# Rotary queries kept in memory as eight blocks of 128 rows, written in four parts, in place of two blocks of four times 128 rows

## The chip, the cores and the metric

The kernel runs on one core of a Trainium2 chip. The metric is the device time of one launch in microseconds. Three runs of the kernel before gave 2459.61, 2461.49 and 2461.84 us; the median is 2461.49 us. The profiled execution took 2459.21 us.

## The reference, cut to what matters

One step of a two-layer decoder on 1024 prompt tokens and 64 sample tokens (8 sequences of 8). Layer A mixes by pooling; layer B attends to one shared latent of 256 numbers and one rotary key of 64 numbers per token. Each of the 8 heads has a query of two parts: 128 numbers without position (the latent is multiplied to match) and 64 rotary ones.

```python
cq = _rmsnorm(u @ w_dq, q_norm)
q = jnp.einsum('btr,rhe->bthe', cq, w_uq)
q_lat = jnp.einsum('bthn,rhn->bthr', q[..., :QK_NOPE], w_uk)
return q_lat, _rope(q[..., QK_NOPE:], pos)
...
s = (jnp.einsum('bqhr,bkr->bhqk', q_lat, c)
     + jnp.einsum('bqhe,bke->bhqk', q_rope, kr)).astype(jnp.float32) * SM_SCALE
```

The prompt's queries attend causally to the prompt; the sample's queries attend to 8 pages of 128 cached tokens each, and to their own tokens. Everything is in float32.

## The kernel before, in words

All activations lie with features on the 128 partitions and tokens on the free axis; the 1088 tokens are cut into chunks of 384, 384 and 320 (`CH`). Matrix products run as three passes of split float32 numbers, a rounded high part and the rest as a low part (`mm3`, lines 188 to 190). A `Plan` holds the list of steps, and loads weight pieces into a ring ahead of their use (`load_piece`, lines 157 and 168). The tile framework places every semaphore. Nearly all DMAs are issued by SyncE (SP), in the order of the program, and SP waits at an issue until what it needs is there; ScalarE issues a few of its own (line 930).

`qkv_phase` computes the shared latent and key, the query's low rank part, and then the queries. `qnope(hh, c, w)` makes one head's no-position query for one chunk: VectorE multiplies the product by the reciprocal norm into an `hl` tile (line 753; four buffers), and SP writes it to memory, to `qn_d[hh]` (line 755). `qrope(g, c, w)` makes the rotary queries of four heads (group `g`) for one chunk. Its two products hold, on 128 partitions, 32 frequencies of each of four heads; VectorE turns them (lines 774 to 784) and leaves in one slab (`hid`) the four parts high 1, low 1, high 2, low 2. In the view `v` a partition is head and frequency, the next axis `q` is the part, the last is the token. Line 787 writes all of `v` with one DMA to `q2_d[g]`, and line 789 writes the sample's tokens to `qs_d`. There are two groups and three chunks, so line 787 runs six times, one `qrope` before every fourth `qnope`. Line 700 writes the reciprocal norms of the low rank parts as a row, and line 701 reads it back to all partitions.

`attention_phase` takes head after head. `rotary(hh)` (lines 863 to 865) loads a tile `q2` (two buffers) of 128 partitions by 1024 tokens: four parts of 32 frequencies of one head. The load is the helper `move` on line 178. It is issued at the start for head 0 and inside `keys(hh)` for the others: `keys(1)` at the start too, the later ones one head ahead, at the third pair of that head's query blocks. `scores` (line 877) multiplies the no-position query with the head's keys, and `q2` with the rotary keys. The sample's attention is put between these steps: `sample_start` loads its queries (`kth<-qns_d` on line 941, `raw<-qs_d` on line 178), `fetch` (lines 978 and 979) loads pages of the cache into `craw` (three buffers), ScalarE and VectorE split them (lines 146 and 147), and `sample_scores`, `sample_turn`, `sample_values` and `sample_mix` work on them.

```python
q2_d = [dpool.tile([4, P, SEQ], F32, name=f"q2_d{g}") for g in range(2)]
...
nc.sync.dma_start(out=q2_d[g][:, :, o:o + m].rearrange("q p t -> p q t"), in_=v[:, :, :m])
...
move(A["q2", hh], q2_d[hh // 4][:, 32 * (hh % 4):32 * (hh % 4) + 32, :])
```

In the profile, buffer numbers are left out of names: `q_d` is `q2_d`, and `q` is the tile `q2`.

Of the kernel before, what the change touches and what calls it, by code (L numbers as in the profile page):

```python
# [11 lines left out]
F32 = mybir.dt.float32  # L12
# [8 lines left out]
P = 128  # L21
D = 1024
KT = D // P
SEQ = 1024
# [9 lines left out]
H = 8  # L34
# [78 lines left out]
def kernel(ctx: ExitStack, tc: tile.TileContext, io: dict):  # L113
    nc = tc.nc

    def pool(name, bufs=1, **kw):
        return tc.tile_pool(name=name, bufs=bufs, **kw)
# [3 lines left out]
    dpool = ctx.enter_context(pool("dpool", space=DRAM))  # L121
# [11 lines left out]

    h = []
    qn_d = [dpool.tile([P, T], F32, name=f"qn_d{i}") for i in range(H)]
    q2_d = [dpool.tile([4, P, SEQ], F32, name=f"q2_d{g}") for g in range(2)]
    cn_d = dpool.tile([NS, 2 * KR], F32, name="cn_d")
    qs_d = dpool.tile([4, 2 * P, NS], F32, name="qs_d")
    qns_d = [dpool.tile([P, 4, NS], F32, name=f"qns_d{g}") for g in range(2)]
# [37 lines left out]
    def move(out, in_):  # L177
        nc.sync.dma_start(out=out.bitcast(F32), in_=in_.bitcast(F32))
# [40 lines left out]
    def slab():  # L219
        return S["hid"].tile([P, 2176], F32R, tag="hid", bufs=5, name="hid")  # L220
# [97 lines left out]
    def lin(c, w, k, m, mo, src=None):  # L318
        n = CH[c][1]
        wh, wl = (x.rearrange("p (k m) -> p k m", k=k) for x in w)  # L320
        ps = bank()[:, :n]
        x = src or U[c]
        mm3(ps, [(wh[:, i, mo:mo + m], wl[:, i, mo:mo + m], x[i][0], x[i][1]) for i in range(k)])
        return ps
# [328 lines left out]
    def qkv_phase():  # L653
# [109 lines left out]
        def qrope(g, c, w):  # L763

            o, n = CH[c]
            pss = [lin(c, w, 3, P, i * P, E["cq", c]) for i in range(2)]
            s = slab()[:, :5 * n].rearrange("p (k t) -> p k t", k=5)
            x1, h1, z1, t, x2 = (s[:, i, :].bitcast(F32) for i in range(5))
            cos, sin = (E["cs"][:, i, o:o + n] for i in range(2))

            def tt(out, a, b, op):
                nc.vector.tensor_tensor(out=out, in0=a, in1=b, op=op)  # L772

            tt(x1, pss[0], E["r"][:, 1, o:o + n], ALU.mult)
            tt(x2, pss[1], E["r"][:, 1, o:o + n], ALU.mult)
            tt(z1, x1, cos, ALU.mult)
            tt(t, x2, sin, ALU.mult)
            tt(z1, z1, t, ALU.subtract)
            tt(t, x1, sin, ALU.mult)
            tt(x2, x2, cos, ALU.mult)  # L780
            tt(x2, x2, t, ALU.add)
            for z, hi in ((z1, 1), (x2, 3)):
                nc.scalar.copy(out=s[:, hi, :], in_=z)
                tt(s[:, hi + 1, :], z, s[:, hi, :].bitcast(F32), ALU.subtract)
            m = min(n, SEQ - o)
            v = s[:, 1:5, :].bitcast(F32)
            nc.sync.dma_start(out=q2_d[g][:, :, o:o + m].rearrange("q p t -> p q t"), in_=v[:, :, :m])
            if m < n:
                nc.sync.dma_start(out=qs_d[:, g * P:(g + 1) * P, :].rearrange("q p t -> p q t"), in_=v[:, :, m:])

# [12 lines left out]
        for i, (hh, c) in enumerate(nopes):  # L803
            if i % 4 == 0:
                g, cc = ropes.pop(0)
                plan.add(lambda w, g=g, c=cc: qrope(g, c, w), uqr[g])
            plan.add(lambda w, hh=hh, c=c: qnope(hh, c, w), uqn[hh // 2])
# [3 lines left out]
    def attention_phase():  # L811
        A = {}
# [5 lines left out]
        def tl(shape, dt, tag, bufs=1):  # L818
            return A["p"].tile(shape, dt, tag=tag, bufs=bufs, name=tag)
# [4 lines left out]
        def start():  # L824
            st = open_scope("att")
            A["p"] = st.enter_context(pool("pa", reuse_waits="tile"))
            A["ps"] = st.enter_context(pool("pps", space=PSUM, reuse_waits="tile"))
            A["c"], A["k2"] = S["cl"], S["k2"]
            for shape, dt, tag, bufs in (
                    ([P, 3, 2, PAGE], F32R, "kth", 2), ([P, 3, 2, PAGE], F32R, "ktl", 2), ([P, PAST + TS], F32, "sp", 1),  # L830
                    ([P, KR], F32, "sa", 1), ([P, SEQ], F32R, "kh", 2), ([P, SEQ], F32R, "kl", 2),
                    ([P, SEQ], F32R, "q2", 2), ([P, 9, 2, NS], F32R, "tt", 1),
                    ([P, 2 * KR], F32R, "cb", 1), ([P, 2, 3 * P], F32, "craw", 3), ([P, 2, 2, KR], F32R, "vt", 2), ([P, 2, 512], F32R, "qz0", 1),
                    ([P, 2, 512], F32R, "qz1", 1), ([P, NB, H, TS], F32R, "sq2", 1), ([P, 2, 512], F32, "att", 1)):
                tl(shape, dt, tag, bufs)
            rotary(0)
            A["mask"] = tl([P, P], F32, "mask")
            nc.sync.dma_start(out=A["mask"], in_=io["mask"])
# [11 lines left out]
        def keys(hh, w):  # L850
            wh, wl = (x.rearrange("p (s k n) -> p s k n", s=2, k=2)[:, 0] for x in w)
            ms = slice((hh % 2) * P, (hh % 2) * P + P)
            kh, kl = tl([P, SEQ], F32R, "kh", 2), tl([P, SEQ], F32R, "kl", 2)
            for half in range(2):
                cs = slice(half * 512, half * 512 + 512)
                ps = one()
                mm3(ps, [(wh[:, k, ms], wl[:, k, ms], A["c"][k][0][:, cs], A["c"][k][1][:, cs]) for k in range(2)])
                split(kh[:, cs], kl[:, cs], ps)
            A["k", hh] = (kh, kl)
            if hh:  # L860
                rotary(hh)

        def rotary(hh):
            A["q2", hh] = tl([P, SEQ], F32R, "q2", 2)
            move(A["q2", hh], q2_d[hh // 4][:, 32 * (hh % 4):32 * (hh % 4) + 32, :])

        def scores(hh, m, qq, q):
            W = P * (2 * m + qq + 1)
# [536 lines left out]
```

## Time and profile before

| | before |
|---|---|
| median of 3 runs | 2461.49 us |
| profiled execution | 2459.21 us |
| its span, first to last instruction | 2457.4 us |
| mean granted TensorE clock | 0.981 |
| TensorE matmul busy (PE) | 2382.0 us, 97% |
| VectorE busy (DVE) | 1232.5 us, 50% |
| ScalarE busy (ACT) | 830.8 us, 34% |
| DMA moved | 186.54 MB |

The span leaves out 1.81 us of the profiled execution's time. Times in rows are microseconds from the start of the span unless marked ns. A busy PE is not PE at its peak, because matmuls overlap each other and run at the clock that is granted. SP is all sequencer: its rows are issues of DMAs and waits.

### The profile page before, as it was taken

How to read it: one execution, taken by the hardware profiler on the slowest of the kernel's cores; microseconds unless marked ns; L12 is line 12 of the kernel's file. 1: busy time of each engine (PE TensorE's matmuls, PEld its weight loads, DVE VectorE, ACT ScalarE, POOL GpSimd, SP SyncE). 2: the span in 40 equal slices, each digit the busy share in tenths (PEclk: the TensorE clock that was granted, in tenths of full speed). 3: DMA queues.
4: the chain of work that ended last, by engine and by line, in shares of the span. 5: the costliest groups of instructions: out<-in, count | busy, mean ns of one | idle time of the engine just before them, and what ended most of it. 6: DMA issues, size and time to landing. Idle time of an engine off the chain costs nothing.

```text
span 2457.4 us, 35907 instructions
## 1 busy us (share of the span) xinstructions
PE 2382.0 (97%) x14516; PEld 2328.5 (95%) x14516; DVE 1232.5 (50%) x2427; ACT 830.8 (34%) x1557; POOL 36.5 (1%) x37
## 2 busy tenths in 40 slices
PE   8999999999999999998998999999999999999996
PEld 7999999999999999997887899999999999999996
DVE  6943333333333668385776774533333333334755
ACT  6622121121121434325666653412112112123422
POOL 0300000000000000000000000000000000000001
PEclk8999999999999999998998999999999999999998
DMA  8411111111111143265433352211111111111202
GB/s 267 119 55 43 44 52 44 43 43 44 45 50 43 43 136 134 50 211 156 121 112 96 98 189 73 58 47 52 44 43 44 43 45 51 43 44 44 63 27 76
DMA packets 96701, 186.54 MB, mean 76 GB/s; under 512 B 18248, under 2 KB 68616, under 8 KB 95759
## 3 DMA queue, kind: packets, MB, share of 16 engines
q1 hardware_dynamic: 90151, 179.78, 23.5%
q10 hardware_dynamic: 6384, 4.47, 0.6%
q8 instruction: 114, 1.87, 0.3%
q14 instruction: 52, 0.43, 0.1%
HBM read 155.00 MB, written 28.85 MB: 75 GB/s over the span
## 4 chain that ended last, share of the span: by engine, by line
PE 85%; DVE 6%; DMA 5%; ACT 1%; issue 1%; SPq 1%; POOL 0%; DVEq 0%; ACTq 0%; POOLq 0%
PE mm L188 26%; PE mm L190 26%; PE mm L189 26%; PE s L877 2%; DMA craw<-in_cache 2%; PE one L927 1%; PE one L992 1%; DVE hid L772 1%; PE one L904 1%; DMA q<-q_d 1%; DVE ul L151 0%; PE mm L459 0%; DMA kth<-qns_d 0%; PE mm L269 0%; DVE h L487 0%
## 5 line engine op out<-in xcount | busy, mean ns | idle before, releaser
L188 PE MATMUL mm<-uh,whi 128*128 128x384 f32 (+1 forms) x2460 | 808.1, 329 | 11.9 <-ACT whi L146 6.2
L189 PE MATMUL mm<-ul,whi 128*128 128x384 f32 (+1 forms) x2460 | 806.1, 328 | 0.0
L190 PE MATMUL mm<-uh,wlo 128*128 128x384 f32 (+1 forms) x2460 | 806.0, 328 | 0.0
L190 PE MATMUL mm<-hid,wlo 128*128 128x384 f32 (+1 forms) x1584 | 517.3, 327 | 0.0
L188 PE MATMUL mm<-hid,whi 128*128 128x384 f32 (+1 forms) x1584 | 517.1, 326 | 0.0
L189 PE MATMUL mm<-hid,whi 128*128 128x384 f32 (+1 forms) x1584 | 516.7, 326 | 0.0
L188 PEld LDWEIGHTS mm<-uh,whi 128*128 128x128 f32 x2460 | 465.1, 189 | 19.9 <-ACT whi L146 6.5
L189 PEld LDWEIGHTS mm<-ul,whi 128*128 128x128 f32 x2460 | 465.3, 189 | 0.4 <-DVE ul L147 0.3
L190 PEld LDWEIGHTS mm<-uh,wlo 128*128 128x128 f32 x2460 | 465.2, 189 | 0.3 <-DVE wlo L147 0.2
L146 ACT CAST whi<-raw 128x1024 fp32r<-128x1024 f32 (+3 forms) x184 | 190.9, 1038 | 756.4 <-PE mm L189 743.2
L314 DVE TENSOR_TENSOR h<-h,mm 128x384 f32<-128x384 f32 (+1 forms) x408 | 216.5, 531 | 419.7 <-PE mm L190 416.3
L188 PEld LDWEIGHTS mm<-hid,whi 128*128 128x128 f32 x1584 | 297.3, 188 | 3.8 <-issue 3.8
L190 PEld LDWEIGHTS mm<-hid,wlo 128*128 128x128 f32 x1584 | 297.3, 188 | 0.0
L189 PEld LDWEIGHTS mm<-hid,whi 128*128 128x128 f32 x1584 | 297.2, 188 | 0.0
L147 DVE TENSOR_TENSOR wlo<-raw,whi 128x1024 fp32r<-128x1024 f32 (+3 forms) x184 | 222.1, 1207 | 74.8 <-ACT whi L146 74.6
L548 DVE SCALAR_TENSOR_TENSOR t<-mm,r 128x384 f32<-128x384 f32 (+1 forms) x192 | 102.7, 535 | 295.0 <-PE mm L190 293.6
L550 ACT ACTIVATE t<-t 128x384 f32<-128x384 f32 (+1 forms) x192 | 97.0, 505 | 391.9 <-DVE t L548 391.9
L147 DVE TENSOR_TENSOR hid<-t,hid 128x384 fp32r<-128x384 f32 (+1 forms) x192 | 102.5, 534 | 141.9 <-ACT hid L146 141.8
L258 ACT ACTIVATE sq<-h 128x384 f32<-128x384 f32 (+1 forms) x126 | 63.4, 506 | 125.5 <-DVE h L314 58.7
L146 ACT CAST hid<-t 128x384 fp32r<-128x384 f32 (+1 forms) x192 | 95.1, 495 | 6.1
L259 DVE TENSOR_TENSOR acc<-acc,sq 128x384 f32<-128x384 f32 (+1 forms) x111 | 60.7, 547 | 42.1 <-ACT sq L258 41.4
L151 DVE SCALAR_TENSOR_TENSOR ul<-h,gains,uh 128x384 fp32r<-128x384 f32 (+1 forms) x96 | 58.3, 631 | 4.5 <-ACT uh L150 4.5
(206 smaller groups left out, 2026.4 us busy)
## 6 DMA issues: line engine op xcount, KB each, us to landing
raw<-in_w_up SPq DMA_DIRECT2D x64, 512.0 KB
raw<-in_w_down SPq DMA_DIRECT2D x64, 512.0 KB
craw<-in_cache SPq DMA_DIRECT2D x64, 192.0 KB
raw<-in_w_gate SPq DMA_DIRECT2D x16, 512.0 KB
craw<-in_cache SPq DMA_DIRECT2D x64, 128.0 KB
h<-in_x_prompt SPq DMA_DIRECT2D x8, 512.0 KB
raw<-qn_d SPq DMA_DIRECT2D x8, 512.0 KB
q<-q_d SPq DMA_DIRECT2D x8, 512.0 KB
```

The costliest lines, as they stand in the source:

```text
L146: nc.scalar.copy(out=hi, in_=x)
L147: nc.vector.tensor_tensor(out=lo, in0=x, in1=hi.bitcast(F32), op=ALU.subtract)
L151: nc.vector.scalar_tensor_tensor(out=lo, in0=x, scalar=g, in1=hi.bitcast(F32), op0=ALU.mult, op1=ALU.subtract)
L188: nc.tensor.matmul(out=out, lhsT=wh, rhs=xh, start=i == 0, stop=False)
L189: nc.tensor.matmul(out=out, lhsT=wh, rhs=xl, start=False, stop=False)
L190: nc.tensor.matmul(out=out, lhsT=wl, rhs=xh, start=False, stop=i == last)
L258: nc.scalar.activation(s, x, AF.Square)
L259: (add or nc.vector).tensor_tensor(out=acc, in0=acc, in1=s, op=ALU.add)
L314: nc.vector.tensor_tensor(out=h[c][:, dt, :], in0=h[c][:, dt, :], in1=ps, op=ALU.add)
L548: nc.vector.scalar_tensor_tensor(out=r, in0=ps, scalar=0.0, in1=R[c], op0=ALU.max, op1=ALU.mult)
L550: nc.scalar.activation(r, r, AF.Square)
L877: nc.tensor.matmul(out=st[:, a, :seg], lhsT=l[:, qs], rhs=r[:, ks], start=i == 0, stop=i == 4)
```

## The change

The rotary queries in memory become eight tiles, one for each head, of 128 rows by 1024 tokens; a row is part and frequency. In place of one DMA, `qrope` issues four, one for each head of the group: from 32 partitions, four parts each, to that head's tile. `rotary` loads a head's whole tile. The sample's write (line 789) stays as it was.

```diff
-    q2_d = [dpool.tile([4, P, SEQ], F32, name=f"q2_d{g}") for g in range(2)]
+    q2_d = [dpool.tile([P, SEQ], F32, name=f"q2_d{i}") for i in range(H)]
...
             v = s[:, 1:5, :].bitcast(F32)
-            nc.sync.dma_start(out=q2_d[g][:, :, o:o + m].rearrange("q p t -> p q t"), in_=v[:, :, :m])
+            for i in range(4):
+                nc.sync.dma_start(
+                    out=q2_d[4 * g + i][:, o:o + m].rearrange("(q p) t -> p q t", q=4),
+                    in_=v[32 * i:32 * i + 32, :, :m])
...
         def rotary(hh):
             A["q2", hh] = tl([P, SEQ], F32R, "q2", 2)
-            move(A["q2", hh], q2_d[hh // 4][:, 32 * (hh % 4):32 * (hh % 4) + 32, :])
+            move(A["q2", hh], q2_d[hh])
```

## Rows read from the trace of the kernel before

**Rows 1.** The page: busy time of the engines, and the chain that ended last.

```profile
PE 2382.0 (97%) x14516; PEld 2328.5 (95%) x14516; DVE 1232.5 (50%) x2427; ACT 830.8 (34%) x1557; POOL 36.5 (1%) x37
...
PE 85%; DVE 6%; DMA 5%; ACT 1%; issue 1%; SPq 1%; POOL 0%; DVEq 0%; ACTq 0%; POOLq 0%
PE mm L188 26%; PE mm L190 26%; PE mm L189 26%; PE s L877 2%; DMA craw<-in_cache 2%; PE one L927 1%; PE one L992 1%; DVE hid L772 1%; PE one L904 1%; DMA q<-q_d 1%; DVE ul L151 0%; PE mm L459 0%; DMA kth<-qns_d 0%; PE mm L269 0%; DVE h L487 0%
```

**Rows 2.** The issues on the rotary queries: duration ns min/median/max, first and last start.

```profile
L178 SPq DMA_DIRECT2D q<-q_d x8: 551/611/631, 1105.1 to 1363.3; - x8
L787 SPq DMA_DIRECT2D q_d<-hid x6: 370/376/433, 1048.1 to 1100.8; - x6
```

**Rows 3.** Busy time by stretch: the sum of the seven stretches with a read.

```profile
core 0: us, PE busy (x) PEld busy (x) DVE busy (x) ACT busy (x) POOL busy (x), PEclk, DMA share, GB/s
...
sum 111.00, PE 81.35 PEld 71.32 DVE 58.28 ACT 53.15 POOL 0.00; mean PE 11.62 PEld 10.19 DVE 8.33 ACT 7.59 POOL 0.00
```

**Rows 4.** The same view: two of the seven stretches between them, and their sum.

```profile
1122.00:1152.00 30.00, 28.41 (x172) 25.59 (x172) 22.29 (x45) 23.90 (x47) 0.00 (x0) 0.84 0.59 181
...
1210.00:1236.00 26.00, 25.77 (x168) 23.16 (x167) 21.05 (x41) 20.00 (x42) 0.00 (x0) 0.95 0.36 112
...
sum 233.00, PE 226.75 PEld 205.06 DVE 179.77 ACT 166.54 POOL 0.00; mean PE 32.39 PEld 29.29 DVE 25.68 ACT 23.79 POOL 0.00
```

**Rows 5.** Waits of PE, 1035 to 1450 us: total us, times, longest.

```profile
PE one L904 <- ACT sp L1030: 4.8, 1, 4.8
...
PE one L188 <- DVE hl L753: 1.6, 1, 1.6
PE one L1046 <- DVE sp L1042: 1.5, 1, 1.5
```

**Rows 6.** The chain that ended last, in order of time: start us, us, what.

```profile
1073.12 4.78 DMA raw<-qn_d
...
1093.14 6.63 DMA qn_d<-hl
...
1191.36 12.76 DMA q<-q_d
...
1272.42 2.30 DMA craw<-in_cache
...
1282.33 9.26 DMA craw<-in_cache
```

**Rows 7.** Timeline of PE: start us, us, instruction, idle time before it and its releaser.

```profile
1114.21 0.79 PE L877 MATMUL s<-k,q 128*128 128x256 f32 x2 [2.68 <-DMA q<-q_d]
...
1120.44 0.88 PE L964 MATMUL one<-kth,whole 128*128 128x64 f32 x3 [3.51 <-DMA kth<-qns_d]
```

**Rows 8.** Busy time by stretch: two of 4 us; the last columns are DMA share and GB/s.

```profile
1073.00:1077.00 4.00, 4.00 (x25) 4.00 (x24) 3.83 (x10) 1.06 (x3) 0.00 (x0) 1.00 1.05 396
1328.00:1332.00 4.00, 2.04 (x19) 1.80 (x16) 0.52 (x2) 0.09 (x1) 0.00 (x0) 1.00 0.26 95
```

**Rows 9.** The stage's half-clock stretches, PE alone: first and sum of six, and one other.

```profile
1113.58:1130.65 17.07, 12.92 (x53) 0.50 0.43 124
...
sum 40.97, PE 32.95; mean PE 5.49
...
1151.13:1154.54 3.41, 3.41 (x19) 0.50 0.38 93
```

**Rows 10.** Timeline of SP: two issues behind the first write, and a later read.

```profile
1049.29 0.90 SPq L755 DMA_DIRECT2D qn_d<-hl  x1
1051.84 1.59 SPq L700 DMA_DIRECT2D row<-y  x2
...
1223.12 0.33 SPq L168 DMA_DIRECT2D raw<-qn_d  x1
```

**Rows 11.** Waits of SP, 1040 to 1106 us.

```profile
SPq L755 <- DVE hl L753: 17.6, 11, 2.6
```

**Rows 12.** Timeline of VectorE, around 1100 us.

```profile
1099.86 0.49 DVE L753 TENSOR_TENSOR hl<-mm,hid 128x320 f32<-128x320 f32 x1 [1.88 <-DMA qn_d<-hl]
```

## The prediction

> **What bounds the kernel now.** I read the page first. TensorE (PE) is busy for 97% of the span, and the chain that ended last lies 85% on it; DMA holds 5% of that chain, 1% of it by name on reads of the rotary queries [rows 1]. So a change of a copy can only pay where PE waits. I then cut the attention stage, 1106 to 1450 us, at the eight reads of the rotary queries, issued between 1105.1 and 1363.3 us [rows 2]. The reader is to compare two sorts of stretch. The seven that begin with such a read (from 1106, 1152, 1191, 1236, 1280, 1323 and 1363 us, each 13 to 19 us long; the first holds two reads) last 111 us in all, and PE is busy in them for 81.35: 29.65 us idle [rows 3]. The seven between them last 233 us with PE busy for 226.75: 6.25 us idle [rows 4]. The names in PE's own list of waits mislead here: its longest is put down to a ScalarE copy [rows 5], but that engine stood behind page loads: behind a read the chain of waits shows a page transfer of 9.26 us, beside 2.30 us for an undisturbed one, and the read itself with 12.76 us [rows 6].
>
> Why the reads are slow: a read moves 512 KB (128 x 1024 x 4 bytes). The one of 1105.1 us released PE at 1114.21, 9.1 us after its issue [rows 2, 7]; the one of 1191.36 took 12.76 us; a read of the same 512 KB from the no-position queries took 4.78 us [rows 6]. In four such microseconds the DMA engines are busy for only 0.26 of their time, at 95 GB/s, where another stretch has them full at 396 GB/s [rows 8]. 0.26 x 16 = 4.2: a read is at work on about four of the sixteen engines, and a transfer behind it that needs all sixteen must wait for those four.
>
> TensorE's clock adds to it. After most of these stalls the granted clock stands at 0.50 (1.2 of 2.4 GHz) for 3.4 to 17 us [rows 9].
>
> **The change part by part.**
>
> *The read.* Its source turns from four blocks of 32 rows into 128 rows in one block, the form of the no-position read. Between the bounds of 4.78 and 12.76 us I take 4.78, the same size with the same two forms. A no-position read, issued at 1223.12 [rows 10], stands also in the stretch from 1210 us, in which PE idles for 0.23 us [rows 4]. If the stretches behind the reads become like the others, 111 us hold 111 x 6.25/233 = 3.0 us of idle time, and 29.65 - 3.0 = 26.6 us go; I take 26. Bounds: 29.65 (all goes), and 13 if half of it has another cause.
>
> *The clock.* Six of the seven half-clock stretches begin at or after a read's stall; the one at 1151.13 us lies before its read and is left out. The six hold 32.95 us of PE work [rows 9], which at the full clock takes half: 16.5 us. Since one dip in seven came after a wait of only 1.5 us (PE one L1046 [rows 5]), some will stay. I take three quarters, 12.4 us; bounds 4 and 16.5.
>
> *The writes.* Six writes become 24 of 32 partitions each, so SyncE issues 18 more. A write's issue takes 0.376 us [rows 2]: 18 x 0.376 = 6.8 us more on SP. In that stage, 1040 to 1106 us, SP waits 17.6 us for VectorE's products of line 753 alone [rows 11], which covers it where the wait comes right behind. Each group of four delays what is queued behind it by 3 x 0.376 = 1.1 us: latent outputs, the no-position writes that give back the four hl buffers, the row of the low-rank norms (line 700). Behind the first write SP's issues end at 1049.29 + 0.90 = 1050.19, and that row goes out at 1051.84 [rows 10], so 1.1 us fits. Two places are exposed. VectorE waited 1.88 us before 1099.86 for a no-position write that was issued at 1093.14, right behind the fifth write, and PE 1.6 us for VectorE [rows 5, 6, 12]; and after the sixth the queue runs on over the sample queries to the rotary reads and the kth reads, for which PE waited until 1120.44 [rows 7]. 2 x 1.1 = 2.2 us. The bytes and the 512 row pieces of a group stay the same, but the pieces of one issue come from a quarter of the partitions. No row shows a large transfer of that kind. It can gain nothing, since nothing is issued earlier; at worst each group is as slow as the narrow read, 12.76 - 4.78 = 8.0 us more. Nearest is the present write, with the same pieces, so I take 0.8 us in all: 3 us lost with the issues. Cover gone, the whole 6.8 us would show.
>
> The Trainium skill speaks against this part: "SBUF — State Buffer", section "Door 1: The DMA port swizzle", says that 32 partitions reach 8 of SBUF's 16 ports, about 218 GB/s. By that page, as an estimate, a group of 768 KB (128 x 4 x 384 x 4 bytes) takes 3.6 us where 396 GB/s gives 2.0 us, and six groups lose up to 10 us instead of my 0.8: the sum would then be 2435 us. The trace of before holds no such transfer, so it neither bears this out nor speaks against it.
>
> *The tiles in memory.* Eight of 128 rows replace two; each head's read waits for the three writes of its own group of heads, as before. The first two reads take heads 0 and 1, whose group is written by the first three of the six writes; the last write, issued at 1100.8 [rows 2], is for heads 4 to 7, read last. No new wait comes of it: nothing.
>
> *Sum.* -26 - 12.4 + 3 = -35.4 us on the profiled execution of 2459.21 us (span 2457.4): 2423.8. The median, 2461.49, lies 2.28 above it, so 2426.1 us.
>
> **The rivals.**
>
> *Part of the stall stays.* VectorE and ScalarE are busy for 22.29 and 23.90 of the 30 us from 1122 [rows 4]; with PE faster, they may become what is late next. Half of the idle time and a quarter of the clock: -13 - 4 + 2 = -15, 2446 us. Against it: from 1210 to 1236 us VectorE is busy for 21.05 of 26, and PE hardly idles [rows 4].
>
> *More goes.* All idle time and all half-clock time of the stage: 29.65 + 6.25 = 35.9, and 16.5 + 1.7 (half of the dip at 1151.13 [rows 9]): -54, 2407 us. Against it: the transposes and splits still alternate between engines.
>
> *The writes stall the projections* (slower). If a 32-partition write ran as narrowly as the present read, each group would hold its queue 8.0 us longer, the four hl buffers would stay full, VectorE's product at line 753 would wait, and PE with it. Six groups: 48 us, and six half-clock dips of at least 3.4 us, each losing half: 10 us more; -38.4 + 58 = +20, 2481 us. It decides once a group loses over 38.4/6 = 6.4 us. Against it: the write's outermost dimension is 32, the read that is slow has 4. The Trainium skill ("DMA: Bandwidth & Descriptors", section "Why a DMA increments its semaphore by 16 and not by 1") takes the largest number of engines up to 16 that divides the slowest dimension of both sides: 4 for the present read, with which the trace's share of 0.26 agrees, and 16 for the new write. By that rule this rival falls.
>
> *The read doesn't speed up*, because its slowness lies in the data and not in the four blocks: only the +3 is left, 2464 us, inside 0.2%. Against it: the same bytes from the neighbouring tensors in 4.78 us.
>
> **How the numbers follow.** 0.2% (4.9 us) is about what a measurement of this kernel can tell from no change. Chances: forecast 0.73, part stays 0.15, more goes 0.06, no speed-up 0.03, stalled projections 0.03. The first three are faster: 0.94; same 0.03; slower 0.03. Around the forecast the bounds reach from 29.65 + 16.5 = 46 us gained (2415) to 26 + 4 - 6.8 = 23 (2438). The range takes in the partial case, 2446, and goes a little beyond the upper gain, to 2412; it leaves out the last two cases, most of "more goes", and tails: under 2 in 10.
>
> **What would show it.** Right: no wait of several us on DMA of the rotary queries in the chain; page loads near 2 to 4 us throughout; PE idle in the stage about 10 us instead of 35.9; two or three half-clock stretches in the stage instead of seven; 24 write issues near 0.37 us; PE's first scores right behind the keys, with no 2.7 us wait. Wrong: idle time behind the reads as before; half clock without stalls; VectorE's line 753 waiting on no-position writes for more than 3 us in all.

## The result, and the profile after

The changed kernel takes 2423.12 us (median of 4 runs, 2420.70 to 2423.21) beside 2460.55 us for the kernel before on the same chip (4 runs, 2453.89 to 2461.84). The ratio is 0.985, with a 95% interval of 0.983 to 0.987: some 37 us less. The forecast was 2426, with a range of 2412 to 2446. The profiled execution of the changed kernel took 2420.70 us, its span 2418.9. In the rows of after, lines behind 787 stand three further down: line 877 is now 880.

The page of after, busy time and the chain that ended last, answers to [rows 1]:

```profile
PE 2363.4 (98%) x14516; PEld 2311.2 (96%) x14516; DVE 1234.7 (51%) x2427; ACT 832.2 (34%) x1557; POOL 36.5 (2%) x37
...
PE 88%; DVE 5%; DMA 3%; ACT 2%; issue 1%; SPq 0%; POOL 0%; DVEq 0%; ACTq 0%; POOLq 0%
```

PE executes the same 14516 matmuls in 18.6 us less busy time (2382.0 before). Nothing was taken from its work, so this is clock. The chain holds 3% DMA where it held 5%.

To see where the time went, take the attention stage in one piece, from the first scores to the last attention product. Busy time by stretch, before and then after; the columns are those of [rows 3]:

```profile
1111.00:1451.00 340.00, 304.11 (x2028) 273.25 (x2026) 236.72 (x480) 217.79 (x470) 0.00 (x0) 0.93 0.40 116
```

```profile
1111.00:1412.00 301.00, 287.11 (x2031) 257.97 (x2029) 238.32 (x480) 217.81 (x470) 0.00 (x0) 1.00 0.42 132
...
1328.00:1332.00 4.00, 4.00 (x31) 3.53 (x30) 2.32 (x4) 2.57 (x4) 0.00 (x0) 1.00 0.83 290
```

Read each row as a sum: length = busy + idle. Before, 340.00 = 304.11 + 35.89; after, 301.00 = 287.11 + 13.89. So 39.0 us went from this one stage: 22.0 us of idle time, and 17.0 us of busy time, with the mean granted clock up from 0.93 to 1.00 (full, 2.4 GHz). Nearly the same number of instructions ran on every engine, and VectorE and ScalarE are busy for nearly as long as before (238.32 and 217.81 us instead of 236.72 and 217.79). The last row stands right behind the last rotary read, issued at 1327.86 us: PE is busy all through, and DMA moves 290 GB/s, where behind the read of [rows 8] it moved 95.

The operations on the rotary queries in after (as [rows 2]), and the page's DMA issues (how many, KB each, us from issue to landing):

```profile
L788 SPq DMA_DIRECT2D q_d<-hid x24: 318/436/1272, 1047.2 to 1101.1; - x24
L178 SPq DMA_DIRECT2D q<-q_d x8: 320/337/520, 1106.9 to 1327.9; - x8
```

```profile
craw<-in_cache SPq DMA_DIRECT2D x64, 192.0 KB, 2.7
craw<-in_cache SPq DMA_DIRECT2D x64, 128.0 KB, 2.1
...
raw<-qn_d SPq DMA_DIRECT2D x8, 512.0 KB, 3.4
q<-q_d SPq DMA_DIRECT2D x8, 512.0 KB, 4.6
```

A rotary read now lands in 4.6 us (the median of eight); one in the chain before took 12.76 [rows 6]. The chain of after between 1106 and 1420 us has no piece on `q_d` at all. What it has of pages is short:

```profile
1160.58 3.69 DMA craw<-in_cache
...
1341.73 4.23 DMA craw<-in_cache
```

where before a page took 9.26 us behind a read [rows 6]. PE's waits, 1035 to 1411 us (as [rows 5]), have lost the single one of 4.8 us:

```profile
PE s L880 <- ACT p L888: 4.4, 7, 1.2
PE mm L188 <- DVE hl L753: 3.8, 2, 3.4
PE one L188 <- DVE hl L753: 1.3, 1, 1.3
PE s L880 <- DMA q<-q_d: 1.3, 1, 1.3
...
PE one L967 <- DMA kth<-qns_d: 0.8, 1, 0.8
```

The first scores still wait for their rotary query, 1.3 us instead of 2.68 [rows 7], and the sample's key products 0.8 us instead of 3.51.

Not everything got shorter. The issues of SP in after that bear on the writes and on the hand-over to attention (start us, us, instruction, how many):

```profile
1047.19 2.26 SPq L788 DMA_DIRECT2D q_d<-hid  x4
...
1099.64 1.88 SPq L788 DMA_DIRECT2D q_d<-hid  x4
...
1102.11 0.50 SPq L158 DMA_DIRECT2D whole<-in_w_ukt  x1
...
1105.42 0.49 SPq L158 DMA_DIRECT2D whole<-in_w_ukt  x1
1105.97 0.72 SPq L168 DMA_DIRECT2D raw<-qn_d  x1
1106.91 0.32 SPq L178 DMA_DIRECT2D q<-q_d  x1
```

and the same two loads of the key weights before:

```profile
1092.23 0.33 SPq L158 DMA_DIRECT2D whole<-in_w_ukt  x1
...
1098.01 0.33 SPq L158 DMA_DIRECT2D whole<-in_w_ukt  x1
```

A group of four writes holds SP for about 2 us; the six take 2.26, 2.67, 1.77, 2.35, 2.44 and 1.88, in all 13.37 us, where the six single issues took 6 x 0.376 = 2.26 [rows 2]. The two weight loads now stand behind the last write, some 10 and 7 us later than before, right ahead of the rotary reads.

### The profile page after: what moved, and what is told of

Same layout as the page of the kernel before. It is cut to its first block, busy times and chain, and to the rows that moved or that the text cites. A ratio compares the mean times of both kernels' runs of the same rounds, so it can differ in the third digit from the quotient of the medians.

```text
span 2418.9 us, 35912 instructions
## 1 busy us (share of the span) xinstructions
PE 2363.4 (98%) x14516; PEld 2311.2 (96%) x14516; DVE 1234.7 (51%) x2427; ACT 832.2 (34%) x1557; POOL 36.5 (2%) x37
## 4 chain that ended last, share of the span: by engine, by line
PE 88%; DVE 5%; DMA 3%; ACT 2%; issue 1%; SPq 0%; POOL 0%; DVEq 0%; ACTq 0%; POOLq 0%
PE mm L188 27%; PE mm L190 26%; PE mm L189 26%; PE s L880 2%; PE one L930 1%; PE one L907 1%; DMA craw<-in_cache 1%; PE one L995 1%; DVE ul L151 0%; PE mm L459 0%; PE one L1067 0%; PE mm L269 0%; DVE hid L772 0%; DVE mx L887 0%; PE one L188 0%
```

## The experiments

**The theories.** The forecast's theory is *width*: a read whose source is four blocks of 32 rows is at work on about four of the sixteen DMA engines, and everything that is issued behind it waits for those. Rivals are *layout* (it is the one contiguous block that makes the read fast) and *late queries* (what stalls PE is only that the scores wait for their own rotary query, not that the read is in the way of others). A third is *order*: with other DMAs to place, the framework puts the instructions in another order (the loads of the key weights above are one case), and the new order alone may be what is faster. For the writes the question is whether 24 narrow ones cost the 3 us of the forecast.

**The old layout, read in four parts.** Six wide writes and the two tiles of before; only the read is split, by its four parts, each from 32 rows to 32 partitions.

```diff
-            move(A["q2", hh], q2_d[hh // 4][:, 32 * (hh % 4):32 * (hh % 4) + 32, :])
+            for q in range(4):
+                move(A["q2", hh][32 * q:32 * q + 32], q2_d[hh // 4][q, 32 * (hh % 4):32 * (hh % 4) + 32, :])
```

Expected:

> The kernel before, with its tiles and its single writes kept, but each head's rotary queries read by four DMAs of 32 rows each instead of one DMA whose source has four blocks outermost. Width theory (one read ran on about four of the sixteen DMA engines and held up everything behind it): the stalls behind the reads go though the layout and the writes are those of before; 24 more issues of about 0.35 us, 8 us, fall on SP in the attention stage, mostly covered: 2420 to 2434 us. Rival, order (the changed number of DMAs made the planner order the instructions anew, and that order is what is faster): 2450 to 2465 unless the order happens to change the same way. Rival, memory layout (contiguous rows are read faster): 2455 to 2465, since the rows lie as before.

Measured: 2417.1 us, ratio 0.983 (0.981 to 0.985), 2.9 us below the expected range. All of the gain is there without the new layout: the tiles in memory are those of before, and each DMA takes one block of 32 rows and a quarter of the bytes. So *layout*, as far as it means the place of the rows in memory, falls. Each of the four reads is contiguous in itself, so this run does not show whether gaps between blocks do harm. The no-position read speaks against that: its 128 rows of 4096 bytes lie 4352 bytes apart (`qn_d` has 1088 columns, 1024 are read), and it lands in 3.4 us. Whether *order* helped is not shown here. Run a second time, beside the changed kernel on one chip:

> Single writes as before and four reads of 32 rows for each head, once more, beside the changed kernel on the same chip. If the changed kernel's 18 more writes cost some 6 us, as the runs of the first calls suggest, it is again 4 to 8 us below the changed kernel; if they cost 1 to 2 us, within 3 us of it.

It gave 2420.04 us, ratio 0.984 (0.983 to 0.985), and the changed kernel there 2421.66. By the words of that expectation the 18 more writes would cost 1 to 2 us; but the comparison is not clean, because the 24 more reads have a price of their own (below). In its trace the 32 reads of 128 KB land in 2.5 us each, in the median.

**The new layout, read as four blocks.** The changed kernel with its tiles padded to 33 rows for each part, so that the read has four blocks of 32 rows as its outermost dimension again. The writes are 24 as after, and the instructions stand in the same order: the traces show it for SP's 246 issues from 1040 us to the end of the stage, and for PE, VectorE and ScalarE within the stage.

```diff
-    q2_d = [dpool.tile([P, SEQ], F32, name=f"q2_d{i}") for i in range(H)]
+    q2_d = [dpool.tile([4, 33, SEQ], F32, name=f"q2_d{i}") for i in range(H)]
...
-                    out=q2_d[4 * g + i][:, o:o + m].rearrange("(q p) t -> p q t", q=4),
+                    out=q2_d[4 * g + i][:, :32, o:o + m].rearrange("q p t -> p q t"),
...
-            move(A["q2", hh], q2_d[hh])
+            move(A["q2", hh], q2_d[hh][:, :32, :])
```

Expected:

> The changed kernel with its 24 writes kept; a head's tile in memory is four blocks of 32 rows with one unused row after each, so that the read has four blocks outermost again. Instructions stand in the same order on every engine as in the changed kernel. Width theory: all that was gained goes, 2455 to 2468 us, with the half-clock stretches back. Order theory: 2423 us, as the order is that of the changed kernel. Writes theory (the single wide write was what disturbed): 2423 us.

Measured: 2466.80 us, ratio 1.0031 (1.0022 to 1.0041). The whole gain is gone, and a little more than that. Its stage by stretch, and 4 us that begin some 6 us behind the issue of its last read but one (1328.68 us):

```profile
1111.00:1457.00 346.00, 302.80 (x2031) 270.86 (x2029) 237.65 (x480) 217.18 (x470) 0.00 (x0) 0.94 0.39 115
1335.00:1339.00 4.00, 0.84 (x8) 0.60 (x6) 0.00 (x0) 0.30 (x1) 0.00 (x0) 0.87 0.18 71
```

and its chain:

```profile
1161.64 10.34 DMA craw<-in_cache
...
1197.15 11.06 DMA q<-q_d
```

The idle time is back (346.00 - 302.80 = 43.2 us), so is the lower clock, and so are page loads of over 10 us and a DMA share of 0.18 (0.18 x 16 = 2.9 engines). Between this kernel and the changed one lies only the padding, and with it the form of the read, and 2466.80 - 2422.87 (the changed kernel's median in the run told next) = 43.9 us. The two ran on different chips, on which the kernel before took 2459.36 and 2459.32 us. As the order is the same and the gain is gone, *order* falls too.

**Half of the heads.** The changed kernel again, beside one in which heads 4 to 7 have the padded tiles and are read as four blocks, heads 0 to 3 as one.

```diff
-            move(A["q2", hh], q2_d[hh])
+            move(A["q2", hh], q2_d[hh] if hh < 4 else q2_d[hh][:, :32, :])
```

Expected of the two:

> The changed kernel once more, as the base for the runs beside it: 2421 to 2425 us.

> The changed kernel, with the tiles of heads 4 to 7 alone as four blocks of 32 rows (narrow reads), heads 0 to 3 as 128 rows. Width theory: four of the eight reads stall, among them neither of the two at the start; about half of 38 us: 2436 to 2446 us. If a single narrow read is enough to upset the order of things, over 2450; if the loss sits in the start of the stage alone, 2423 to 2428.

Measured: the changed kernel 2422.87 us, ratio 0.986 (0.984 to 0.987); with half of the reads narrow 2445.03, ratio 0.994 (0.993 to 0.995). That is 22.2 us more for four narrow reads, half of the 43.9 for eight: about 5.5 us for each read, in the last four as in all eight. The chain has a long page load again behind the first read of the narrow form:

```profile
1225.80 9.87 DMA craw<-in_cache
```

**A slow copy that nobody waits for.** To part *width* from *late queries*: the changed kernel, with one added copy of 512 KB for each head, from the weights to a spare tile in memory that is never read. In one kernel the copy has four blocks of 32 rows on both sides, in the control it is contiguous.

```diff
+    spare_d = [dpool.tile([4, 33, SEQ], F32, name=f"spare_d{i}") for i in range(H)]
...
+            nc.sync.dma_start(out=spare_d[hh][:, :32, :], in_=io["w_up"][0, 4 * hh:4 * hh + 4, 0:32, :])
```

Control:

```diff
+    spare_d = [dpool.tile([P, SEQ], F32, name=f"spare_d{i}") for i in range(H)]
...
+            nc.sync.dma_start(out=spare_d[hh], in_=io["w_up"][0, 4 * hh])
```

Expected:

> The changed kernel with one more copy of 512 KB at each rotary read, from four blocks of 32 rows of a weight to an unused tile in memory of four blocks (both sides have 4 outermost). Nobody waits for it. If the narrow read did harm by holding the engines that other transfers need, this brings most of the loss back: 2440 to 2470 us. If it did harm because the rotary queries themselves came late (PE waits for them), nothing: 2421 to 2430 us.

> The control for the unused narrow copy: the same 512 KB more at each rotary read, from 128 rows of a weight to an unused tile of 128 rows, so 16 engines can share it. Holding theory: 2422 to 2434 us, at any rate well below the narrow copy. If the bytes alone are what counts, as slow as the narrow copy.

Measured: narrow 2447.84 us, ratio 0.996 (0.994 to 0.997); contiguous 2421.34, ratio 0.985 (0.983 to 0.987). But the copies were not where they were meant to be. Their issues, first of the narrow and then of the contiguous ones:

```profile
L870 SPq DMA_DIRECT2D spare_d<-in_w_up x8: 612/636/709, 65.7 to 326.1; - x8
```

```profile
L870 SPq DMA_DIRECT2D spare_d<-in_w_up x8: 489/518/588, 66.7 to 90.9; - x8
```

With nothing to wait for, they were placed early in the program, hundreds of microseconds ahead of attention. So as a test of attention this one missed. It still says something: from 60 to 330 us PE executed 1636 matmuls in the changed kernel, and 1507 with the narrow copies:

```profile
60.00:330.00 270.00, 266.93 (x1636) 264.11 (x1635) 135.45 (x254) 89.79 (x162) 23.05 (x20) 1.00 0.21 64
```

```profile
60.00:330.00 270.00, 254.50 (x1507) 248.59 (x1507) 122.69 (x239) 80.98 (x148) 21.57 (x19) 0.97 0.22 73
```

Eight narrow copies cost 26.5 us (2447.84 - 2421.34, on one chip) more than eight contiguous ones, in a stage that has nothing to do with rotary queries, at a DMA share of 0.22. The contiguous ones, which stood close together at the start of that stage, cost nothing that can be seen; as they stood elsewhere than the narrow ones, they are a control for the bytes and not for the place.

The test was then made where it was meant: each narrow copy is tied to the place right behind a rotary read.

```diff
-            move(A["q2", hh], q2_d[hh])
+            read = nc.sync.dma_start(out=A["q2", hh].bitcast(F32), in_=q2_d[hh])
+            with tc.issue_after(read.ins):
+                nc.sync.dma_start(out=spare_d[hh][:, :32, :], in_=io["w_up"][0, 4 * hh:4 * hh + 4, 0:32, :])
```

Expected, with the changed kernel run a third time beside it:

> The changed kernel with the unused narrow copy of 512 KB (four blocks to four blocks in memory) bound to stand behind each head's rotary read on SP; in the run before it stood elsewhere, in the first 330 us. Holding theory: the stalls come back in the attention stage although nobody waits for the copy: 2440 to 2470 us, PE idle over 25 us there and half-clock stretches again. Lateness theory (only the wait for the rotary queries themselves counted): 2422 to 2430 us.

> The changed kernel, as the base for the runs beside it: 2420 to 2425 us.

Measured: 2456.51 us, ratio 0.998 (0.998 to 0.999), beside 2421.66, ratio 0.984 (0.983 to 0.985): 34.9 us lost to eight copies that nobody reads. Its copies, its stage, its waits of PE and its DMA issues:

```profile
L871 SPq DMA_DIRECT2D spare_d<-in_w_up x8: 635/712/736, 1106.1 to 1381.3; - x8
```

```profile
1110.00:1449.00 339.00, 304.07 (x2031) 273.47 (x2030) 244.70 (x481) 220.19 (x470) 0.00 (x0) 0.94 0.42 129
```

```profile
PE s L883 <- ACT p L891: 15.3, 11, 6.0
...
PE s L883 <- DMA q<-q_d: 1.2, 1, 1.2
```

```profile
craw<-in_cache SPq DMA_DIRECT2D x64, 192.0 KB, 3.5
...
raw<-qn_d SPq DMA_DIRECT2D x8, 512.0 KB, 5.0
q<-q_d SPq DMA_DIRECT2D x8, 512.0 KB, 6.4
```

The stage looks like the one before: 339.00 - 304.07 = 34.93 us idle (35.89 before), clock 0.94 (0.93 before). The rotary reads are the wide ones and go out ahead of the copies, and PE waits for a rotary query only once, 1.2 us (1.3 in after), so *late queries* can hold little of this. The loads around a copy take longer in the median: pages of 192 KB 3.5 us instead of 2.7, no-position queries 5.0 instead of 3.4, rotary reads 6.4 instead of 4.6; pages of 128 KB stay at 2.1. PE's list names ScalarE, as it did before [rows 5]. To see what lies behind such a name, follow its longest wait, 6.0 us, backwards through the timelines of PE, ScalarE, VectorE and SP (start us, us, instruction, idle time before it and its releaser):

```profile
1119.29 0.69 PE L883 MATMUL s<-kh,whi 128*128 128x384 f32 x1 [6.02 <-ACT p L891]
```

```profile
1117.48 1.28 ACT L891 ACT_TABLE_LOAD   x1 [5.39 <-DVE mx L890]
```

```profile
1116.72 0.50 DVE L886 TENSOR_TENSOR s<-s,mask 128x128 f32<-128x128 f32 x2 [3.25 <-DMA mask<-in_mask]
```

```profile
1106.07 0.72 SPq L871 DMA_DIRECT2D spare_d<-in_w_up  x1
1106.84 0.43 SPq L842 DMA_DIRECT2D mask<-in_mask  x1
```

The mask of the scores was issued right behind the spare copy and released VectorE 1116.72 - 1106.84 = 9.9 us later; VectorE's maximum, ScalarE's exponential and PE's next scores stood behind it. *Width* is what the runs support: the harm of a narrow transfer is that it is in the way. No contiguous copy was bound to the same place, so what the bytes alone cost there is not shown; at the 396 GB/s of [rows 8] eight times 512 KB would take 10.6 us, as an estimate, if nothing overlapped them, and 34.9 were lost. Is a narrow transfer in the way among the DMA engines, or because SP issues in order and waits? For the mask it was not SP, which issued it 0.05 us behind the end of the copy's issue: the transfer itself came late. For the other loads these runs do not part the two.

**The price of the writes.** Twice the writes: the 24 are issued a second time, to a second set of tiles that is never read.

```diff
-            for i in range(4):
+            for d, i in [(q2_d, i) for i in range(4)] + [(q3_d, i) for i in range(4)]:
                 nc.sync.dma_start(
-                    out=q2_d[4 * g + i][:, o:o + m].rearrange("(q p) t -> p q t", q=4),
+                    out=d[4 * g + i][:, o:o + m].rearrange("(q p) t -> p q t", q=4),
```

Expected:

> The changed kernel with the 24 writes of 32 partitions issued twice, the second time to eight unused tiles. It prices the writes: my term of 3 us for 18 more issues predicts 3 to 5 us more, about 2427 us; if writes are hidden, 2422 to 2424; if 32 partitions run at half the rate, as the Trainium skill's page "SBUF — State Buffer" has it, about 10 us more for the narrow transfers, 2433; if the issues are not covered at all, 24 x 0.38 = 9 us more, 2432.

Measured: 2427.51 us, 4.6 more than the changed kernel's 2422.87. The runs of the two (2424.76 to 2431.72, and 2419.14 to 2425.42) just overlap, so the size of this is known to a few microseconds only. The first group of eight holds SP for 5.48 us.

**The writes on ScalarE's queue.** The same 24, issued by ScalarE instead of SP.

```diff
-                nc.sync.dma_start(
+                nc.scalar.dma_start(
```

Expected:

> The changed kernel with the 24 writes issued by ScalarE's queue in place of SP's. If SP's issues cost the 2 to 3 us that the prediction charged, they come back: 2419 to 2422 us. If they are hidden, 2423; if ScalarE's splits and copies wait behind the issues, 2424 to 2432.

Measured: 2427.52 us, ratio 0.987 (0.986 to 0.988), again 4.6 more than 2422.87: a miss as an improvement. The last of them goes out late, at 1111.8 us instead of 1101.1, and the first rotary read with them, at 1113.0 instead of 1106.9. And PE waits for a split that stands behind them. The issues, PE's longest wait there, and the last issues in ScalarE's timeline:

```profile
L788 ACTq DMA_DIRECT2D q_d<-hid x24: 309/444/1064, 1046.2 to 1111.8; - x24
L178 SPq DMA_DIRECT2D q<-q_d x8: 331/332/451, 1113.0 to 1337.7; - x8
```

```profile
PE one L188 <- DVE vl L147: 7.9, 1, 7.9
```

```profile
1103.01 9.12 ACTq L788 DMA_DIRECT2D q_d<-hid  x8
```

This is the third case of the expectation. ScalarE's half of the values' split comes behind its last eight issues, VectorE's half behind ScalarE's, and PE waits 7.9 us for it, a wait that after does not have. A queue that is freer on paper is of no use when its engine comes to the issue later and its own work waits behind the issues.

**Six wide writes and one wide read.** If the width of the read is what pays and the 18 more issues are what it costs, a layout that needs neither should beat both kernels. Here a partition of the product holds frequency and head, head innermost, instead of head and frequency. The tile of a group is head, part, frequency, token; one write from all 128 partitions fills four heads, and a head's 128 rows lie in one block. The weights are permuted ahead of the launch to match, with a second table of cosines and sines that repeats each row four times; the kernel loads it after the shared key is turned. The sample's load is rearranged to match (not shown).

```diff
-    q2_d = [dpool.tile([4, P, SEQ], F32, name=f"q2_d{g}") for g in range(2)]
+    q2_d = [dpool.tile([4, 4, 32, SEQ], F32, name=f"q2_d{g}") for g in range(2)]
...
-            nc.sync.dma_start(out=q2_d[g][:, :, o:o + m].rearrange("q p t -> p q t"), in_=v[:, :, :m])
+            nc.sync.dma_start(out=q2_d[g][:, :, :, o:o + m].rearrange("h q f t -> f h q t"), in_=v[:, :, :m])
...
-            move(A["q2", hh], q2_d[hh // 4][:, 32 * (hh % 4):32 * (hh % 4) + 32, :])
+            move(A["q2", hh], q2_d[hh // 4][hh % 4].rearrange("q f t -> (q f) t"))
```

Expected:

> One write of 128 partitions for each group and chunk, and one read of 128 contiguous rows for each head: frequency outside head on the partitions of the query's rotary products (weights and a second table of cosines laid out for it on the host side, the table loaded over the first once the keys are turned). 18 fewer issues than the changed kernel, 24 fewer than with four reads, one more load of 1.1 MB. If the writes cost the changed kernel 6 us, 2414 to 2418 us, as with four reads; if the new load or 32 outermost with 16 inside is slower, 2420 to 2428.

Measured: 2411.94 us (2409.26 to 2414.45), ratio 0.981 (0.979 to 0.982), 2.1 us below the expected range. It beats the changed kernel of the same chip (2417.61 to 2424.42) by 2421.66 - 2411.94 = 9.7 us. Its issues:

```profile
L178 SPq DMA_DIRECT2D q<-q_d x8: 331/332/433, 1103.4 to 1320.7; - x8
L787 SPq DMA_DIRECT2D q_d<-hid x6: 592/597/682, 1046.1 to 1098.1; - x6
```

Six writes of 0.6 us hold SP for 3.6 us, and the first rotary read goes out at 1103.4 instead of 1106.9.

**Where the writes' price lies.** Three times can be read from each profile: the first product of line 685 (the norm ahead of the queries, one line further down where lines were added), the first and the last of the score products with the rotary queries, and the span. Of after, the two rows are:

```profile
L685 PE MATMUL mm<-hl,ones x6: 430/483/484, 1022.2 to 1040.9; 128*1 128x384 f32 x4, 128*1 128x320 f32 x2
```

```profile
L880 PE MATMUL s<-k,q x192: 274/337/419, 1113.4 to 1401.5; 128*128 128x384 f32 x48, 128*128 128x512 f32 x48, 128*128 128x256 f32 x32, 128*128 128x320 f32 x32
```

so that 1113.4 - 1022.2 = 91.2 us lie ahead of the scores and 1401.5 - 1113.4 = 288.1 in them, and 2418.9 - 1401.5 = 1017.4 remain. In the same way:

| kernel | writes | reads | ahead of the scores | scores | rest |
|---|---|---|---|---|---|
| before | 6 | 8 narrow | 91.7 | 326.3 | 1016.9 |
| after, three profiles | 24 | 8 | 91.2, 93.9, 91.8 | 288.1, 286.1, 287.8 | 1017.4, 1016.2, 1017.6 |
| new layout, four blocks | 24 | 8 narrow | 95.1 | 329.3 | 1014.5 |
| old layout, four reads, two profiles | 6 | 32 | 88.3, 88.7 | 290.0, 290.3 | 1016.1, 1016.1 |
| six writes, wide read | 6 | 8 | 87.9 | 285.0 | 1013.8 |
| 24 writes twice | 48 | 8 | 99.7 | 288.2 | 1017.5 |
| writes by ScalarE | 24 | 8 | 101.9 | 286.6 | 1016.0 |

Of most kernels there is one profile, and the three of after lie 2.7 us apart ahead of the scores, so differences of 3 us there are rough. At equal reads, 24 writes for 6 cost 95.1 - 91.7 = 3.4 us ahead of the scores with narrow reads, and 92.3 (the mean of three) - 87.9 = 4.4 with wide ones; another 24 cost 99.7 - 92.3 = 7.4. The wide read gives back 95.1 - 92.3 = 2.8 of it there, because the first scores wait for a read. In the scores, 24 more read issues (the old layout) cost about 290 - 287 = 3 us, and over whole runs the wide read with six writes is 2420.04 - 2411.94 = 8.1 us faster than the four reads with six writes. The rest varies by 3 us between profiles for the same work, as does the time ahead of line 685 (1020.5 to 1023.9 us), so a part of the 9.7 us that lies there is put down to nothing.

## Why the prediction was right

**The sum.** Forecast -35.4 us, measured 2423.12 - 2460.55 = -37.4. The place was right too: one stage gave it all, and the trace after it is as long as before (1016.9 and 1017.4 us in the table).

**The read.** That a read from one block would land like the no-position read was right: 4.6 us for 4.78. That the width of the source is the cause was argued from a DMA share, and the experiments show it: with the blocks back everything is lost, with four reads of one block each everything is gained, and narrow copies that nobody reads do most of the same harm (34.9 of 43.9 us). By the Trainium skill ("DMA: Bandwidth & Descriptors", section "Why a DMA increments its semaphore by 16 and not by 1") four outermost blocks leave a transfer on four engines; the share of 0.18 to 0.26 behind a narrow read agrees, and so does the padded tile, in which only that dimension and the gaps changed.

The idle time was sized too high: 22.0 us went instead of 26. The step took it that stretches with a read would become like those between, at 6.25 us in 233. But the new stage idles 13.89 us in 301, at a rate of 4.6% where 6.25/233 is 2.7%. Some of that is the hand-over, 1.3 and 0.8 us; some is what the partial rival named, ScalarE's exponentials (line 888) behind which the scores now wait, 4.4 us in seven waits where it was 1.7 in four. That rival was right in kind and small.

**The clock.** Sized too low: 17.0 us less busy time instead of 12.4. The step kept a quarter of the half-clock time because one dip in seven had come after a short wait. None was kept, the mean granted clock of the stage is 1.00, though waits of up to 1.3 us are still there. The two errors, 4.0 us too much and 4.6 too little, cancel, and that is luck. The padded tile shows a second pair of the same kind over whole runs: the form of the read is worth 43.9 us where 26 + 12.4 = 38.4 were forecast, and the writes cost 7.4 (below) where 3 were.

**The writes.** The size was near ahead of the scores: +3 forecast, 3.4 to 4.4 us by the table. Over whole runs the term was too small by more than half, and the working behind it was wrong in part. An issue was taken at 0.376 us; the median is 0.436 and the longest 1.272, so SP holds 13.37 - 2.26 = 11.1 us more and not 6.8. Of the two exposed places the first did not lose: VectorE's wait at line 753 for a no-position write, 1.88 us [rows 12], went down to 0.55, and stands in after as

```profile
1099.59 2.19 DVE L753 TENSOR_TENSOR hl<-mm,hid 128x384 f32<-128x384 f32 x4 [0.55 <-DMA qn_d<-hl]
```

Nor did that stage lose much by other waits: from 1020 to 1106 us PE waits 5.8 us before (3.4, 1.6 and 0.8) and 5.8 in after (3.8, 1.3 and 0.7; 7.2 and 6.5 in its other two profiles). With more writes it is the right place: with the writes doubled, PE waits 6.7 and 5.3 us for the same products of VectorE (line 754 there). The chain of after does put VectorE's turning at line 772 (at 1089.13 us) behind one of the four writes from its slab (from 1085.50, 3.30 us long). But in VectorE's timeline there is no idle time ahead of that instruction, so no loss is shown there:

```profile
1084.59 3.48 DVE L772 TENSOR_TENSOR hid<-hid 128x384 f32<-128x384 f32 x7
1087.99 1.22 DVE L147 TENSOR_TENSOR wlo<-raw,whi 128x1024 fp32r<-128x1024 f32 x1
1089.13 0.55 DVE L772 TENSOR_TENSOR hid<-hid 128x384 fp32r<-128x384 f32 x1
```

The second place, the hand-over behind the sixth group, was right: the first rotary read goes out at 1106.9 us instead of 1105.1, 1.8 us later where 1.1 was forecast. The wait for that read shows a good part of the price. It is 2.68 us before and 5.07 in the new layout with four blocks, 2.4 of the 3.4 us; it is absent with six writes and the wide read, and 1.3, 2.3 and 1.3 in the three profiles of after, on average 1.6 of the 4.4. What was not seen at all are the two weight loads that now stand behind the last write:

```profile
1105.42 5.35 DMA whole<-in_w_ukt
```

Before, each of them had gone out ahead of one of the last two writes; now the 5.35 us of the second are in the chain. That the tiles in memory move nothing was right even so: with the same eight tiles and the writes on ScalarE's queue, SP issues the two loads at 1092.20 and 1097.98 us, as before. So it is the writes in SP's queue, and not the tiles, that move them. Over whole runs the price is larger than ahead of the scores: 2466.80 - 2459.36 = 7.4 us between four blocks and the kernel before on the same chip, and 9.7 between after and the single wide write. What the further 4 to 5 us are, stays open; the profiled executions of four blocks and of the single wide write are the fastest of their runs, and the first, at 2462.57 us, holds only 3.4 of the 7.4. So does how much of the price is the number of issues, how much the 32 partitions of each, and how much the other order in which SP comes to its issues: no run here had few narrow writes, or four wide ones in place of a group. Landing times in after point both ways: writes of 192 KB take 3.2 us from 32 partitions and 2.0 from 128 (line 755), writes of 128 KB 2.6 and 4.6. The Trainium skill's page "SBUF — State Buffer", section "Door 1: The DMA port swizzle", gives the rate from which the forecast worked out 10 us, as an estimate, for the partitions alone. The runs do not decide that: 7.4 to 9.7 us as a whole is near it, but holds the issues too, and doubling the same writes cost only 4.6.

**The rivals.** *Writes that stall the projections* did not come: PE's waits on line 753 are 5.1 us in after (3.8 and 1.3), and 3.4 + 1.6 = 5.0 before. *The read doesn't speed up* fell with 4.6 us. *More goes* was half right, for the clock. **The signs named beforehand:** no rotary read in the chain of the stage, short page loads, and no wait of 2.7 us came as said; idle time was 13.9 and not 10, no half-clock stretch was left instead of two or three, and the issues were longer than 0.37.

## What to carry to other kernels

Look at the outermost dimension of a large DMA's source and target: with only four there, eight reads of 512 KB cost 44 us here, and eight copies that nobody reads cost 34.9, so most of it, as far as these runs show, is not their own lateness but that of what was issued behind them; splitting each along that dimension, or one block for all, takes it back. A layout fix that multiplies issues pays some back: put the permutation into the weights if you can, so that both the write and the read stay whole (9.7 us faster here). And when a trace blames another engine for PE's wait, follow that engine's own wait back to a load, and see what was issued ahead of the load.

## What the runs showed that was not expected

- Issues that follow one another at once are not all alike: 318 ns for the shortest of the 24 writes, 436 in the middle, 1272 for the longest; a group of four takes 1.8 to 2.7 us, one of eight 5.48.
- A narrow copy with no reader and no waiter costs most of what a needed one costs, 34.9 us for eight, and 26.5 us for eight in another stage, while eight contiguous copies of the same size, close together in that other stage, cost nothing.
- The clock paid for nearly as much as the waits: of 39.0 us, 17.0 are the same matmuls at full instead of half clock.
